# A decoder layer on one core: the first two block products of each gate and up pair are put ahead of the plain group before them, and the x loads get the priority of weight loads

## The chip, the cores and the metric

The kernel runs on one core of a Trainium2 chip. The metric is device time in microseconds; lower is better. A core has a matrix engine (TensorE, PE in the profile, with its weight loads as PEld), a vector engine (DVE), a scalar engine (ACT), GpSimd (POOL) and a sync engine (SP) that here issues most of the DMA transfers. Each engine works through its own instructions in the order in which the program has them; semaphores order them across engines.

## The reference

One layer on 256 tokens of width 2048, all in float32:

```
x = x + 0.5 * swiglu(rms_norm(x), ffn1 gate, up, down)     # 2048 -> 5632 -> 2048
x = x + hybrid_mixer(rms_norm(x), ...)                     # dilated attention || gated linear attention
x = x + cross_attention(rms_norm(x), rms_norm(mem), ...)
x = x + 0.5 * swiglu(rms_norm(x), ffn2 gate, up, down)

def swiglu(h, w_gate, w_up, w_down):
    return (jax.nn.silu(h @ w_gate) * (h @ w_up)) @ w_down
```

The change is in the two feed-forward blocks (FFN) and in one helper at the start. The mixer and the cross-attention between them stay as they are.

## The kernel before, in words

**Precision.** A float32 operand is held as a high part and a low part, both of type float32r. `split` (lines 137 to 139) makes them of a weight tile: ACT copies the tile to `wh`, DVE subtracts `wh` from it and writes `wl`. A product is then three matmuls: high by high, high by low, low by high. Activations are split the same way (`xTh` and `xTl`, `hTh` and `hTl`).

**Groups.** A weight matrix is read in tiles of 1 MB, 128 rows by 4 x 512 columns: four k blocks of one chunk of 512 output columns. One such tile used in the ordinary way is called a plain group here: `wgroup` loads and splits it, `mm3` (lines 160 to 168) does 4 k blocks x 2 token tiles x 3 = 24 matmuls. `proj` runs all the groups of a chunk one after the other.

**Pairs.** For chunk f = 0 of an FFN gate and up are two ordinary projections. For the other ten chunks `strassen` (line 201) computes gate and up of the chunk together. The k blocks of groups 0 and 1 of both matrices form a 2 x 2 block product (two token tiles by gate and up), done with seven block products (`product`, lines 191 to 199, 12 matmuls each) in place of eight. For that, weight tiles are added to each other: on DVE (`add`, line 215) and by DMA transfers that accumulate, which GpSimd issues (`accumulate`, line 219). `sums` (`sh`, `sl`) are the sums of activations, made once per FFN. Groups 2 and 3 of both matrices follow as four plain groups. PE's order in a pair is:

| step | matmuls | what |
|---|---|---|
| H1 (into `x`) | 12 | gate tile of group 0 |
| H2 (into `y`) | 12 | that tile plus the up tile of group 0 |
| turn of the chunk before | 8 transposes | its `h` becomes `hT` |
| P3 to P6 | 4 x 12 | further sums, up and gate tiles |
| G2 | 24 | gate, group 2 |
| P7 | 12 | last sum |
| U2, G3, U3 | 3 x 24 | up group 2, gate group 3, up group 3 |

Then ACT applies silu to gate (`sg`, line 375) and DVE multiplies with up (`h`, line 386).

**Parts.** The 11 chunks go in parts of 4, 4 and 3 (`PARTS`). After each part its `hT` tiles go through the down projection: four output chunks of 4, 4 or 3 plain groups. So two parts in each FFN begin with a pair behind a down projection.

**Buffers.** The split tiles `wh` and `wl` lie in rings of three buffers each. Loaded tiles (`raw`) have six buffers in two pools that take turns. In the accumulators' memory the tags `acc` and `ps` have four buffers each; H1 and H2 use `ps`, P4 and P6 accumulate into `acc`.

**What sets the order.** A planner orders each engine's instructions when the program is built, by the order of the code and by priorities: what stands in `tc.high_priority(200)` (`WPRI`: weight loads, splits, copies of the pairs) is moved forward as if it stood 200 instructions earlier. `later` and `tick` put off transposes by a number of products. Nothing is chosen at run time: an instruction that waits holds up all behind it on its engine.

**Start.** `load_x` (lines 444 to 450) reads the four 512 KB pieces of x, squares them on ACT and makes `r1`, the scale by which the norm is applied after the projection; silu of chunk 0 needs it. Its loads have priorities of 170, 136, 102 and 68.

## Time and profile before

| what | us |
|---|---|
| median of 3 runs | 1942.17 (1941.89 to 1942.6) |
| the profiled execution's own time | 1941.39 |
| its span, first to last instruction | 1939.6 |
| PE busy | 1920.4 (99%) |
| PE weight loads busy | 1584.2 (82%) |
| DVE busy | 1258.6 (65%) |
| ACT busy | 976.4 (50%) |
| GpSimd busy | 88.6 (5%) |

The 1.8 us between the profiled execution's time and its span lie around the instructions. Times in the profile count from the span's start. A recorded matmul of 512 columns lasts 0.39 us, and the next one can start while it still runs, so the distance from start to start shows more than the busy share. The first FFN lasts up to about 724 us, the second from about 1226 us to the end. The table of waits gives engine, tile and line, whom it waited for, and then total us, number of times and the longest; `xN` at a row's end merges N instructions of one kind.

### The profile page before, as it was taken

The page shows a single profiled execution, that of the slowest core. Times are in us where ns is not written, and L with a number is a line of the kernel's source. Part 1 is how long each engine was busy: PE and PEld are TensorE (multiplying, and loading weights), DVE is VectorE, ACT ScalarE, POOL GpSimd, SP SyncE. Part 2 cuts the span into 40 slices and gives each one's busy share as a digit, 9 for nine tenths or more (in the row PEclk, how much of TensorE's full clock was granted, in tenths as well). Part 3 has the DMA queues.
Part 4 walks back from the last instruction along what each step waited for, and adds up shares of the span by engine and source line. Part 5 has one row for each costly group of instructions (what it writes and reads, how often), then busy time and mean ns, then how long its engine had stood idle before and what let it go on. Part 6 is the DMA issues. An engine that isn't in the chain of part 4 may idle for free.

```text
span 1939.6 us, 21252 instructions
## 1 busy us (share of the span) xinstructions
PE 1920.4 (99%) x8760; PEld 1584.2 (82%) x8760; DVE 1258.6 (65%) x956; ACT 976.4 (50%) x881; POOL 88.6 (5%) x95
## 2 busy tenths in 40 slices
PE   9999999999999999999999999999999999999999
PEld 7888878888878888778888889888887888887887
DVE  7776477775578565446775555777646777557863
ACT  6555345553355446444566445555534555335642
POOL 0000000000000000012220000000000000000000
PEclk9999999999999999999999999999999999999999
DMA  9767557775477734445456553667755777556771
GB/s 380 247 220 282 188 177 264 270 250 195 152 236 249 274 127 156 158 162 190 174 217 217 176 193 132 253 224 239 260 195 154 264 269 268 194 174 217 238 290 57
DMA packets 63292, 416.13 MB, mean 215 GB/s; under 512 B 7099, under 2 KB 8251, under 8 KB 14428
## 3 DMA queue, kind: packets, MB, share of 16 engines
q1 hardware_dynamic: 55996, 370.22, 50.0%
q0 software_dynamic: 5760, 41.95, 10.5%
q10 hardware_dynamic: 1440, 2.62, 0.4%
q8 instruction: 68, 1.11, 0.2%
q14 instruction: 28, 0.23, 0.0%
HBM read 370.72 MB, written 2.10 MB: 192 GB/s over the span
## 4 chain that ended last, share of the span: by engine, by line
PE 73%; DVE 16%; ACT 6%; issue 4%; POOL 0%; DMA 0%; ACTq 0%; SPq 0%; DVEq 0%
PE acc L167 20%; PE acc L168 20%; PE acc L166 20%; DVE wl L139 11%; ACT wh L138 5%; PE x L197 4%; DVE raw L215 4%; PE x L167 1%; PE x L168 1%; PE x L166 1%; PE acc L197 1%; DVE acc L241 1%; DVE h L386 1%; PE y L197 1%; PE tp L313 0%
## 5 line engine op out<-in xcount | busy, mean ns | idle before, releaser
L139 DVE TENSOR_TENSOR wl<-raw,wh 128x2048 fp32r<-128x2048 f32 (+2 forms) x410 | 917.5, 2258 | 578.3 <-ACT wh L138 577.5
L138 ACT CAST wh<-raw 128x2048 fp32r<-128x2048 f32 (+2 forms) x410 | 762.9, 1886 | 646.2 <-PE acc L168 463.4
L166 PE MATMUL acc<-wh,xTh 128*128 128x512 f32 x1024 | 401.5, 394 | 7.2 <-ACT wh L138 7.2
L167 PE MATMUL acc<-wl,xTh 128*128 128x512 f32 x1024 | 401.1, 392 | 4.4 <-DVE wl L139 4.3
L168 PE MATMUL acc<-wh,xTl 128*128 128x512 f32 x1024 | 399.3, 390 | 0.0
L166 PE MATMUL acc<-wh,hTh 128*128 128x512 f32 x704 | 274.7, 390 | 0.0
L168 PE MATMUL acc<-wh,hTl 128*128 128x512 f32 x704 | 274.0, 389 | 0.0
L167 PE MATMUL acc<-wl,hTh 128*128 128x512 f32 x704 | 273.9, 389 | 0.0
L167 PEld LDWEIGHTS acc<-wl,xTh 128*128 128x128 f32 x1024 | 192.7, 188 | 50.8 <-DVE wl L139 11.9
L166 PEld LDWEIGHTS acc<-wh,xTh 128*128 128x128 f32 x1024 | 192.1, 188 | 49.5 <-ACT wh L138 9.4
L168 PEld LDWEIGHTS acc<-wh,xTl 128*128 128x128 f32 x1024 | 192.6, 188 | 39.8
L168 PEld LDWEIGHTS acc<-wh,hTl 128*128 128x128 f32 x704 | 132.1, 188 | 27.4
L166 PEld LDWEIGHTS acc<-wh,hTh 128*128 128x128 f32 x704 | 132.2, 188 | 27.2
L167 PEld LDWEIGHTS acc<-wl,hTh 128*128 128x128 f32 x704 | 132.2, 188 | 27.2
L215 DVE TENSOR_TENSOR raw<-raw 128x2048 f32<-128x2048 f32 x40 | 91.5, 2287 | 0.7
L219 POOL DMA_DIRECT2D raw<-raw x40 | 34.6, 865 | 1187.9 <-DVE raw L215 975.9
L167 PE MATMUL x<-wl,xTh 128*128 128x512 f32 x160 | 62.3, 389 | 0.0
L168 PE MATMUL x<-wh,xTl 128*128 128x512 f32 x160 | 62.3, 389 | 0.0
L166 PE MATMUL x<-wh,xTh 128*128 128x512 f32 x160 | 62.2, 389 | 0.0
L231 ACT COPY acc<-x 128x512 f32<-128x512 f32 x20 | 11.4, 571 | 95.6 <-PE x L197 95.6
L166 PE MATMUL acc<-wh,mTh 128*128 128x512 f32 x128 | 50.1, 392 | 0.0
L168 PE MATMUL acc<-wh,mTl 128*128 128x512 f32 x128 | 49.8, 389 | 0.0
(301 smaller groups left out, 1934.3 us busy)
## 6 DMA issues: line engine op xcount, KB each, us to landing
raw<-in_ffn_w_up_dram SPq DMA_DIRECT2D x88, 1024.0 KB, 7.7
raw<-in_ffn_w_down_dram SPq DMA_DIRECT2D x88, 1024.0 KB, 5.0
raw<-in_ffn_w_gate_dram SPq DMA_DIRECT2D x85, 1024.0 KB, 7.1
raw<-in_w_in_dram SPq DMA_DIRECT2D x48, 1024.0 KB, 4.8
raw<-raw POOLq DMA_DIRECT2D x40, 1024.0 KB, 6.9
raw<-in_w_out_dram SPq DMA_DIRECT2D x16, 1024.0 KB, 4.7
raw<-in_xattn_w_k_dram SPq DMA_DIRECT2D x4, 1024.0 KB, 5.2
raw<-in_xattn_w_q_dram SPq DMA_DIRECT2D x4, 1024.0 KB, 4.7
```

The costliest lines, as they stand in the source:

```text
L138: SC.copy(wh, src)
L139: last_split[:] = [V.tensor_sub(wl, src, wh.bitcast(F32)).ins]
L166: PE.matmul(acc[t], lh, wh, start=first and i == 0, stop=False, skip_group_check=seeded)
L167: PE.matmul(acc[t], lh, wl, start=False, stop=False, skip_group_check=seeded)
L168: PE.matmul(acc[t], ll, wh, start=False, stop=last and i == len(half) - 1, skip_group_check=seeded)
L197: PE.matmul(acc, lhs(k)[i], w[:, k], start=first, stop=j == 1 and k == 3, skip_group_check=not start)
L215: V.tensor_add(dst, x, y)
L219: G.dma_start(dst, x, accum_op=ALU.add)
L231: SC.copy(c0l, x)
L241: V.tensor_sub(c0r, ys, x)
L386: V.scalar_tensor_tensor(h, upv[t], r[:, t:t + 1], sg[t], op0=ALU.mult, op1=ALU.mult)
```

## The change

`strassen` is cut in two. `head` does the four loads, H1, H2 and the copies of their results, and returns a function `rest` that does P3 to U3. A caller can hand `ahead` to `proj` or `rest`: it is called just before the last plain group is written, and starts the head of the next pair there. That last group is U3 of the pair before, the last up group of chunk 0, or the last down group of a part. The last pair of a part has no such call; the down projection behind it makes it. The x loads go from their four priorities to `WPRI`.

```diff
-XPRI = 170
...
     def strassen(Wl, cl, Wr, cr, lhs, ab, sums, groups):
 
+        state = head(Wl, cl, Wr, cr, lhs, ab, sums)
+        return state(groups)
+
+    def head(Wl, cl, Wr, cr, lhs, ab, sums):
+
         a, b = ab
         ral, rar = load(Wl, cl, a), load(Wr, cr, a)
         rbr, rbl = load(Wr, cr, b), load(Wl, cl, b)
...
         x, y = PM([P, 512], "x"), PM([P, 512], "y")
-        c0l, c0r, c1r = (pa.tile([P, 512], F32, tag="acc", name="acc") for _ in range(3))
+        c0l = pa.tile([P, 512], F32, tag="acc", name="acc")
         product(x, of(a, 0), parts(ral), True)
...
-        add(ral, ral, rbr)
-        product(x, s_(1), parts(ral), False)
...
+        def rest(groups, ahead=None):
+            c0r, c1r = (pa.tile([P, 512], F32, tag="acc", name="acc") for _ in range(2))
+            add(ral, ral, rbr)
+            product(x, s_(1), parts(ral), False)
...
+            accs = ((c0l, x), (c0r, c1r))
+            for i, g in enumerate(groups):
+                for acc, W, c in zip(accs, (Wl, Wr), (cl, cr)):
+                    if ahead and acc is accs[1] and i == len(groups) - 1:
+                        ahead()
+                    for h, half in enumerate(wgroup(W, c, g)):
+                        mm3(acc, lhs, half, False, i == len(groups) - 1 and h == 1, seeded=True)
+                        tick()
+                    if i == 0 and W is Wl and c == cl:
+                        product(x, of(b, 1), parts(ral), False)
+            return accs
+
+        return rest
...
-    def proj(W, c, lhs, groups, fine=None, last=False):
+    def proj(W, c, lhs, groups, fine=None, last=False, ahead=None):
...
         for i, g in enumerate(groups):
+            if ahead and i == len(groups) - 1:
+                ahead()
...
+        def begin(f):
+            heads[f] = head(wg, f, wu, f, lhs_x, (0, 1), sums)
+
         for part in PARTS:
             for f in part:
+                ahead = (lambda f=f: begin(f + 1)) if f + 1 in part else None
...
-                    gate, upv = strassen(wg, f, wu, f, lhs_x, (0, 1), sums, (2, 3))
+                    gate, upv = heads.pop(f)((2, 3), ahead)
...
-                    upv = proj(wu, f, lhs_x, range(4))
+                    upv = proj(wu, f, lhs_x, range(4), ahead=ahead)
...
             for c in range(NC):
-                acc = proj(wd, c, lhs_h, part, last=last and end and c == NC - 1)
+                ahead = (lambda: begin(part[-1] + 1)) if c == NC - 1 and not end else None
+                acc = proj(wd, c, lhs_h, part, last=last and end and c == NC - 1, ahead=ahead)
...
-            with tc.high_priority(XPRI - 34 * c):
+            with tc.high_priority(WPRI):
                 SY.dma_start(xs[c], A["x"][0, :, c * 512:(c + 1) * 512].rearrange("(t p) d -> p t d", p=P))
```

Three places show what the planner makes of it. First DVE from chunk 2 to chunk 3 of the first FFN, before. `wl_962` is the split of G3, `wl_992` of U3, `wl_1041` and `wl_1060` of H1 and H2, `wl_1095` of P3, `wl_1112` of P4; the L215 rows are the two adds, the `h` rows the multiplication with up:

```order
L139 TENSOR_TENSOR wl_962<-raw_959,wh_961 128x2048
L139 TENSOR_TENSOR wl_992<-raw_989,wh_991 128x2048
L139 TENSOR_TENSOR wl_1041<-raw_1027,wh_1040 128x2048
L215 TENSOR_TENSOR raw_1027<-raw_1027,raw_1029 128x2048
L139 TENSOR_TENSOR wl_1060<-raw_1027,wh_1059 128x2048
L386 SCALAR_TENSOR_TENSOR h_1023<-acc_760,r1_323,sg_1019 128x512
L386 SCALAR_TENSOR_TENSOR h_1025<-acc_761,r1_323,sg_1021 128x512
L215 TENSOR_TENSOR raw_1027<-raw_1027,raw_1031 128x2048
L139 TENSOR_TENSOR wl_1095<-raw_1027,wh_1094 128x2048
L139 TENSOR_TENSOR wl_1112<-raw_1033,wh_1111 128x2048
```

And now; `wl_962` is G3 again, `wl_1001` and `wl_1020` are H1 and H2, `wl_1040` is U3, `wl_1079` P3, `wl_1096` P4:

```order
L138 TENSOR_TENSOR wl_962<-raw_959,wh_961 128x2048
L138 TENSOR_TENSOR wl_1001<-raw_989,wh_1000 128x2048
L219 TENSOR_TENSOR raw_989<-raw_989,raw_991 128x2048
L138 TENSOR_TENSOR wl_1020<-raw_989,wh_1019 128x2048
L219 TENSOR_TENSOR raw_989<-raw_989,raw_993 128x2048
L138 TENSOR_TENSOR wl_1040<-raw_1037,wh_1039 128x2048
L138 TENSOR_TENSOR wl_1079<-raw_989,wh_1078 128x2048
L138 TENSOR_TENSOR wl_1096<-raw_995,wh_1095 128x2048
L405 SCALAR_TENSOR_TENSOR h_1071<-acc_797,r1_323,sg_1067 128x512
L405 SCALAR_TENSOR_TENSOR h_1073<-acc_798,r1_323,sg_1069 128x512
```

U3's split has moved from ahead of H1's to behind the second add, and the `h` rows from ahead of the second add to behind P4's split.

Second SP in the first microseconds, before. `raw_254` is the last gate tile of chunk 0, `raw_347`, `raw_377`, `raw_407` and `raw_437` its up tiles, `raw_471` the first tile of chunk 1:

```order
L132 DMA raw_254<-in_ffn1_w_gate_dram 128x2048
L132 DMA raw_347<-in_ffn1_w_up_dram 128x2048
L448 DMA x0_103<-in_x_dram 128x2x512
L132 DMA raw_377<-in_ffn1_w_up_dram 128x2048
L448 DMA x1_104<-in_x_dram 128x2x512
L132 DMA raw_407<-in_ffn1_w_up_dram 128x2048
L132 DMA raw_437<-in_ffn1_w_up_dram 128x2048
L448 DMA x2_105<-in_x_dram 128x2x512
L132 DMA raw_471<-in_ffn1_w_gate_dram 128x2048
```

And now; `raw_437` to `raw_443` are the four tiles of the head of chunk 1:

```order
L131 DMA raw_254<-in_ffn1_w_gate_dram 128x2048
L468 DMA x0_103<-in_x_dram 128x2x512
L468 DMA x1_104<-in_x_dram 128x2x512
L468 DMA x2_105<-in_x_dram 128x2x512
L468 DMA x3_106<-in_x_dram 128x2x512
L131 DMA raw_347<-in_ffn1_w_up_dram 128x2048
L131 DMA raw_377<-in_ffn1_w_up_dram 128x2048
L131 DMA raw_407<-in_ffn1_w_up_dram 128x2048
L131 DMA raw_437<-in_ffn1_w_gate_dram 128x2048
L131 DMA raw_439<-in_ffn1_w_up_dram 128x2048
L131 DMA raw_441<-in_ffn1_w_up_dram 128x2048
L131 DMA raw_443<-in_ffn1_w_gate_dram 128x2048
```

All four x loads now stand ahead of the first up tile, and the head's four tiles ahead of the last up tile of chunk 0 (the row behind these).

Third ACT at the same time, before, from the last gate cast on. `junk` rows are the squares of x, `sh` rows the casts of the activation sums, `wh_349` and `wh_379` the casts of the first and second up tile:

```order
L138 CAST wh_256<-raw_254 128x1024 x2
L138 CAST wh_349<-raw_347 128x2048
L302 ACTIVATE junk_300,ss1_298<-x0_103 128x512
L302 ACTIVATE junk_302,ss1_298<-x0_103 128x512
L138 CAST wh_379<-raw_377 128x2048
L302 ACTIVATE junk_305,ss1_298<-x1_104 128x512
L302 ACTIVATE junk_307,ss1_298<-x1_104 128x512
L138 CAST sh_329<-sa_335 128x1024
L138 CAST sh_329<-sb_336 128x1024
L138 CAST wh_409<-raw_407 128x2048
```

And now, behind the last gate cast and the squares of x0 and x1:

```order
L315 ACTIVATE junk_310,ss1_298<-x2_105 128x512
L315 ACTIVATE junk_312,ss1_298<-x2_105 128x512
L315 ACTIVATE junk_315,ss1_298<-x3_106 128x512
L315 ACTIVATE junk_317,ss1_298<-x3_106 128x512
L137 CAST sh_329<-sa_335 128x1024
L137 CAST sh_329<-sb_336 128x1024
L394 ACTIVATE sg_325<-acc_128,r1_323 128x512
L394 ACTIVATE sg_327<-acc_129,r1_323 128x512
L137 CAST wh_349<-raw_347 128x2048
L137 CAST wh_379<-raw_377 128x2048
```

The first up cast stood right behind the last gate cast; now eight squares, two casts of sums and the two silus of chunk 0's gate stand between them.

## The prediction

> **Names.** A pair is the gate and up product of one chunk f of 512 hidden columns. In the order of the text before it has seven block products of 12 matmuls (H1 and H2, the ones that move; then P3 to P6; P7 after the first plain group) and four plain groups of 24 (G2, U2, G3, U3). Every weight tile is split first: ACT writes `wh`, DVE writes `wl`, into rings of three buffers.

> **What bounds the kernel now.** The page's first section:

> ```profile
> PE 1920.4 (99%) x8760; PEld 1584.2 (82%) x8760; DVE 1258.6 (65%) x956; ACT 976.4 (50%) x881; POOL 88.6 (5%) x95
> ```

> PE bounds it nearly everywhere, so the change can only win what PE loses between matmuls. The chain of waits shows the undisturbed pace, and the length of a pair:

> ```profile
> 118.31 2.72 PE x L197 x12
> 160.58 2.72 PE x L197 x12
> ```

> Twelve matmuls in 2.72 us is 0.227 us each. The same place comes back after 160.58 - 118.31 = 42.27 us. A pair has 7 x 12 + 4 x 24 = 180 matmuls, 40.8 us, and eight transposes, so somewhat over half a microsecond is lost in it. PE's timeline in chunk 7 shows where:

> ```profile
> 412.05 0.39 PE L166 MATMUL acc<-wh,xTh 128*128 128x512 f32 x1
> 412.28 0.39 PE L166 MATMUL x<-wh,xTh 128*128 128x512 f32 x1
> 412.86 0.50 PE L167 MATMUL acc<-wl,xTh 128*128 128x512 f32 x1 [0.19 <-DVE wl L139]
> 413.19 0.39 PE L168 MATMUL acc<-wh,xTl 128*128 128x512 f32 x1
> ```

> This is the start of G2. The start at 412.86 comes 0.58 us after the one before it, 0.35 too late; the next loses 0.11. Together 0.46 us (the profile calls only 0.19 idle, since a recorded matmul lasts 0.39 while the next may start after 0.227). The first pair of a part, which follows a down projection, loses more, here in chunk 4, and the first pair of all loses its share a little earlier, between H2 and P3:

> ```profile
> 284.17 0.39 PE L166 MATMUL x<-wh,xTh 128*128 128x512 f32 x1
> 286.02 0.73 PE L166 MATMUL acc<-wh,xTh 128*128 128x512 f32 x2 [1.47 <-ACT wh L138]
> 286.59 0.40 PE L167 MATMUL acc<-wl,xTh 128*128 128x512 f32 x1
> ...
> 56.67 1.07 PE L197 MATMUL y<-wl,sh 128*128 128x512 f32 x4
> 58.41 0.96 PE L197 MATMUL x<-wh,sh 128*128 128x512 f32 x3 [0.67 <-ACT acc L231]
> ```

> Chunk 4: 286.02 - 284.17 - 0.23 = 1.62, and 0.11 behind it, 1.73 us. Chunk 1: 58.41 - 56.67 - 4 x 0.227 = 0.83, with 0.11 behind it 0.94 us. The table of waits gives the counts:

> ```profile
> PEld acc L167 <- DVE wl L139: 11.9, 19, 2.0
> PEld acc L166 <- ACT wh L138: 9.4, 6, 2.0
> PE acc L166 <- ACT wh L138: 7.2, 5, 1.6
> ```

> Five waits of PE for `wh`: one is the kernel's first matmul, four are the first pairs of a part (two parts in each FFN). The waits for `wl` hold the 15 ordinary pairs (20 pairs less those four and chunk 1). What the pair waits for is the row of splits, seen on DVE and ACT:

> ```profile
> 384.07 1.91 ACT L138 CAST wh<-raw 128x2048 fp32r<-128x2048 f32 x1 [4.43 <-PE acc L168]
> 390.72 1.91 ACT L138 CAST wh<-raw 128x2048 fp32r<-128x2048 f32 x1 [0.52 <-DVE raw L215]
> ...
> 386.01 2.29 DVE L139 TENSOR_TENSOR wl<-raw,wh 128x2048 fp32r<-128x2048 f32 x1 [3.67 <-ACT wh L138]
> 388.34 2.29 DVE L215 TENSOR_TENSOR raw<-raw 128x2048 f32<-128x2048 f32 x1
> 392.67 2.29 DVE L139 TENSOR_TENSOR wl<-raw,wh 128x2048 fp32r<-128x2048 f32 x1 [2.03 <-ACT wh L138]
> 396.20 2.28 DVE L215 TENSOR_TENSOR raw<-raw 128x2048 f32<-128x2048 f32 x1
> 400.51 4.49 DVE L139 TENSOR_TENSOR wl<-raw,wh 128x2048 fp32r<-128x2048 f32 x2 [2.03 <-ACT wh L138]
> 410.52 6.69 DVE L139 TENSOR_TENSOR wl<-raw,wh 128x2048 fp32r<-128x2048 f32 x3
> ```

> Split, add, split, add, split follow one another (cast to `wl` 1.94, `wl` to add 2.33, add to cast 2.38, cast to `wl` 1.95), and a block product is over in 2.72 us. So the head eats the lead that the plain groups (5.44 us for one 2.29 us split) had built up, and the last `wl` of the row, at 410.52 + 2.3 = 412.8, is late.

> **The change part by part.** No instruction is added or removed on any engine; they change places.

> *H1 and H2 ahead of the last plain group.* Between H2 and P3 there now lie 24 matmuls, 5.44 us. I test whether the row of splits then keeps up. The three-buffer ring lets H1's cast begin when P7 ends. From there on DVE's order (shown above with the change): 1.94 + 2.33 + 2.38 + 1.95 to H2's `wl`, then 2.29 for it, 2.29 for the second add and 2.29 for the `wl` of U3: 15.5 us. PE has U2, G3, H1 and H2 in that time and then one matmul of U3: 3 x 5.44 + 0.23 = 16.6 us. So 1.1 us is to spare at the tightest place. The next ones have more: P3's cast can start at H1's end, and its `wl` ends 4.2 us later, with 8.2 us of PE work between; at G2, where today's stall is, the cast starts at P4's end and `wl` 4.2 us later, with the transposes, P5 and P6 (over 6.2 us) between. The silu results and `h` operations stand after these on ACT and DVE, and the transposes stay behind P4. In a part's first pair the same ring holds, as the last down group takes U3's place. So I count all the stalls as gone: 15 x 0.46 + 4 x 1.73 + 0.94 = 6.9 + 6.9 + 0.9 = 14.8 us. Ends of this term: half of it, 7.4, if the 1.1 us is used up in part; 16.5 if the 0.1 us goes as well by which an ordinary pair is longer than its matmuls, transposes and stall account for (15 x 0.1).

> *Loads.* H's four loads now stand ahead of U3's in SP's queue. A load lands within

> ```profile
> raw<-in_ffn_w_up_dram SPq DMA_DIRECT2D x88, 1024.0 KB, 7.7
> ```

> and U3's takes the buffer of U2, free when U2 is split, before U2's matmuls start; from there to U3's cast PE has U2 and G3, 10.9 us. Cost 0, hidden by these groups; without that cover up to 7.7 us per pair.

> *The x loads.* All four (2 MB in all) now go before the first up group's load, and on ACT their eight squares, the two casts of the sums and the two silus of the first gate stand ahead of the first up group's cast. That cast feeds PE directly:

> ```profile
> 21.65 2.00 ACT L138 CAST wh<-raw 128x1024 fp32r<-128x1024 f32 x2 [0.81 <-DMA raw<-in_ffn_w_gate_dram]
> 24.15 1.91 ACT L138 CAST wh<-raw 128x2048 fp32r<-128x2048 f32 x1 [0.50 <-DMA raw<-in_ffn_w_up_dram]
> 25.96 0.63 ACT L302 ACTIVATE junk<-x 128x512 f32<-128x512 f32 x1
> 31.40 1.06 ACT L138 CAST sh<-sa 128x1024 fp32r<-128x1024 f32 x1
> 56.62 1.25 ACT L375 ACTIVATE sg<-acc,r 128x512 f32<-128x512 f32 x2
> ...
> 25.01 1.22 DVE L180 TENSOR_TENSOR fa<-xTh,xTl 128x1024 f32<-128x1024 f32 x1
> 27.28 2.28 DVE L139 TENSOR_TENSOR wl<-raw,wh 128x2048 fp32r<-128x2048 f32 x1
> 31.40 0.69 DVE L187 TENSOR_TENSOR sb<-fb,sa 128x512 f32<-128x512 f32 x1
> 54.61 0.15 DVE L333 TENSOR_REDUCE r1t<-ss 128x2 f32<-128x8 f32 x1
> ...
> 55.12 0.71 POOL L329 TENSOR_TENSOR r<-r1m,mhalf 128x2 f32<-128x2 f32 x1 [5.51 <-DVE r1m L335]
> ...
> 30.38 0.62 PE L166 MATMUL acc<-wh,xTh 128*128 128x512 f32 x2
> 30.83 0.39 PE L167 MATMUL acc<-wl,xTh 128*128 128x512 f32 x1
> ```

> 1 MB lands in 24.15 - 21.65 = 2.5 us there, so the last x lands near 26.7 and the up group near 29.2. ACT: squares from 23.65 on, 8 x 0.63 = 5.0, to 28.7. DVE: the sums end at 32.1 less the 2.2 us of the up group's `wl`, which now comes later: 29.9; then the reduction up to the end of POOL's power, 55.83 - 54.61 = 1.2: 31.1. ACT meanwhile casts the sums (2 x 1.0, from 29.2 to 31.2), then the silus, 1.15 to the next start: 32.3. The up group's cast ends at 34.2, its `wl` 2.3 us later, 36.6. PE's third matmul of that group starts at 36.6 instead of 30.83: **5.8 us lost**, paid once. It is hidden by nothing, since all later work is behind it. Lower end: the second silu cannot start before the gate's last matmul ends near 30.5; 0.6 + 1.91 + 2.3 later is 35.3, 4.5 us lost. Upper end: x landing 2 us later, 8 us.

> *Sum.* Against the profiled execution (span 1939.6, its own time 1941.39): 1941.4 - 14.8 + 5.8 = 1932.4. The median of the runs shown is 0.8 above the profiled execution, so 1933.2; I say **1933.2**.

> **The rivals.**

> *A, the clock.* In the wait at the start PE stands still from 30.5 to 34.3, 3.8 us. At the kernel's start matmuls ran at half pace:

> ```profile
> 8.24 0.63 PE L168 MATMUL acc<-wh,xTl 128*128 128x512 f32 x1
> 8.66 0.63 PE L166 MATMUL acc<-wh,xTh 128*128 128x512 f32 x1
> ```

> 0.43 instead of 0.227. If the wait brings that back for eight matmuls, 8 x 0.2 = 1.6 us more: 1934.8. For it: no wait in this trace is near 3.8 us; against: behind 284.17, 1.6 us, the pace is full at once. [...] Chance 0.15.

> *B, the stalls move.* The 1.1 us at U3 is partly used up, by hand-over delays that I read from one pair, and half the gain stays: 1942.2 - 7.4 + 5.8 = 1940.6. For it: the margin is 7% of the row. Against: every other link has over 1 us. Chance 0.12.

> *C, slower.* The row of splits between P7 and U3 takes longer than PE's 16.6 us, say because H's loads, now kept over a plain group, come late to the adds. Each microsecond over costs 20 us in 20 pairs; past 0.65 us over (17.2 instead of 15.5) the kernel is slower than 1946. At 1 us over: 1933.2 + 20 = 1953. Against: the buffers they take are free after P6, G2 and P7 at the latest, and from P7's split, ahead of P7's matmuls, to the second add lie over 13 us against 7.7. Chance 0.07.

> **How the numbers follow.** Forecast 0.60, A 0.15, B 0.12, C 0.07, and 0.06 for a cheaper start with a full gain (1942.2 - 16.5 + 4.5 = 1930.2). 0.2% is 3.9 us, about what these runs can tell from no change. Forecast, A and the cheap start are faster by more: 0.81. B lies within 0.2%: 0.12. C: 0.07. The range reaches from just under the cheap start, 1929.5, over the dear one (1942.2 - 14.8 + 8 = 1935.4) with a few stalls left, to 1938.5; about 0.8 lies in it.

> **What would show it.** Right: the pair's 42.27 us becomes about 41.8; no wait of PE for `wh` or `wl` at G2 and none over 0.3 us in a pair; one wait of some 4 us near 30.5 and a shorter one near 35, with the up group's third matmul near 36.6. Wrong: waits for `wl` at U3 about 5 us into the group after H2 (B, C); matmuls 0.43 us apart after 34 (A); PE running through 30 to 36, which would mean that ACT's order does not bind.

## The result, and the profile after

The change takes 1933.19 us (median of 5 runs, 1932.96 to 1933.82) against 1942.17 us before (5 runs, 1941.85 to 1942.6): a ratio of 0.9954, 95% interval 0.994 to 0.9969. The prediction was 1933.2. The profiled execution of the change takes 1933.82 us with a span of 1932.0. That the total agrees does not say that its terms do, so they are taken apart here. In one experiment (e8) two of ten runs took 2879.82 and 9818.56 us; its time below is that of the other eight.

The first section of the changed kernel's page, to be held against the one of before:

```profile
PE 1916.0 (99%) x8760; PEld 1589.1 (82%) x8760; DVE 1265.0 (65%) x956; ACT 981.6 (51%) x881; POOL 90.3 (5%) x95
```

The numbers of instructions are the same. DVE and ACT are busy a few us more with the same work; PE has 4 us less. The chain of waits of the changed kernel (start, length, what):

```profile
67.39 2.72 PE x L196 x12
70.11 2.72 PE acc L196 x12
73.71 2.74 PE x L196 x12
...
109.08 2.72 PE x L196 x12
111.80 2.73 PE acc L196 x12
115.40 2.75 PE x L196 x12
```

The same place comes back after 115.40 - 73.71 = 41.69 us; before it was 42.27. In a pair the chain now runs over PE nearly without a break. The table of waits of the changed kernel (total us, times, longest):

```profile
PE acc L165 <- ACT wh L137: 5.0, 3, 3.1
PE acc L166 <- DVE wl L138: 3.6, 3, 1.6
PE tp L675 <- DVE o L690: 1.1, 1, 1.1
```

The waits of the 15 ordinary pairs for `wl`, of the four part-opening pairs for `wh` and the one in chunk 1 are gone. The waits left for split weights lie in the first 40 us and, one of 1.6 us, at 1230 us at the start of the second FFN; that one is there before the change too. PE's timeline at the start of the changed kernel:

```profile
32.22 0.39 PE L167 MATMUL acc<-wh,xTl 128*128 128x512 f32 x1
35.70 0.88 PE L165 MATMUL acc<-wh,xTh 128*128 128x512 f32 x2 [3.09 <-ACT wh L137]
38.02 0.79 PE L166 MATMUL acc<-wl,xTh 128*128 128x512 f32 x1 [1.44 <-DVE wl L138]
38.62 0.63 PE L167 MATMUL acc<-wh,xTl 128*128 128x512 f32 x1
39.04 0.63 PE L165 MATMUL acc<-wh,xTh 128*128 128x512 f32 x1
39.47 0.63 PE L166 MATMUL acc<-wl,xTh 128*128 128x512 f32 x1
```

Here are the two waits that were foretold, somewhat later than foretold, and behind them matmuls 0.43 us apart, which was rival A.

For one account of all this I added up, from the starts of PE's matmuls, by how much each matmul of a projection or block product is more than 0.227 us ahead of the next start (0.113, half of it, for half-size ones). The table has the sums in us for the profile of each kernel; "later" is everything behind chunk 1, and 11 us of it are the same in every kernel. The lower rows are the experiments below.

| kernel | first gate (chunk 0) | first up (chunk 0) | chunk 1 | later |
|---|---|---|---|---|
| before | 1.8 | 0.0 | 1.3 | 27.7 |
| the change | 4.2 | 7.6 | 0.1 | 11.1 |
| the change, second profile (e10) | 2.2 | 8.0 | 0.1 | 11.1 |
| heads alone (e1) | 1.9 | 0.0 | 5.3 | 11.1 |
| x loads alone (e2) | 1.8 | 7.8 | 0.7 | 27.8 |
| squares behind the first up split (e3) | 2.1 | 2.2 | 1.6 | 11.1 |
| no head ahead of a down projection's end (e4) | 2.4 | 8.4 | 0.1 | 19.2 |
| heads, but none for chunk 1 (e5) | 2.2 | 0.0 | 1.3 | 11.1 |
| short operation behind the second add (e7) | 2.4 | 9.7 | 0.5 | 13.3 |
| long operation there (e8) | 1.9 | 8.0 | 1.6 | 23.4 |

Heads and x loads together gained 27.7 + 1.3 - 11.1 - 0.1 = 17.8 us in the pairs, not 14.8. The start lost 8.4 (second profile) to 10.0 us (first), not 5.8. The two misses cancel in the total; that they do is luck.

### The profile page after: what moved, and what is told of

Same layout as the page of the kernel before. It is cut to its first block, busy times and chain, and to the rows that moved or that the text cites. A ratio compares the mean times of both kernels' runs of the same rounds, so it can differ in the third digit from the quotient of the medians.

```text
span 1932.0 us, 21279 instructions
## 1 busy us (share of the span) xinstructions
PE 1916.0 (99%) x8760; PEld 1589.1 (82%) x8760; DVE 1265.0 (65%) x956; ACT 981.6 (51%) x881; POOL 90.3 (5%) x95
## 4 chain that ended last, share of the span: by engine, by line
PE 96%; DMA 1%; DVE 1%; ACT 1%; POOL 0%; issue 0%; SPq 0%; ACTq 0%; POOLq 0%
PE acc L166 22%; PE acc L167 22%; PE acc L165 22%; PE x L196 11%; PE acc L196 6%; PE y L196 3%; PE x L167 2%; PE x L165 2%; PE x L166 2%; DMA raw<-in_ffn_w_gate_dram 1%; PE tp L366 1%; DVE wl L138 0%; PE tp L326 0%; ACT wh L137 0%; POOL gsr L686 0%
## 5 line engine op out<-in xcount | busy, mean ns | idle before, releaser
L138 DVE TENSOR_TENSOR wl<-raw,wh 128x2048 fp32r<-128x2048 f32 (+2 forms) x410 | 920.4, 2259 | 537.8 <-ACT wh L137 536.4
L166 PE MATMUL acc<-wl,xTh 128*128 128x512 f32 x1024 | 400.7, 391 | 3.6 <-DVE wl L138 3.6
L167 PE MATMUL acc<-wh,xTl 128*128 128x512 f32 x1024 | 400.4, 391 | 0.0
L167 PE MATMUL acc<-wh,hTl 128*128 128x512 f32 x704 | 274.0, 389 | 0.0
L166 PE MATMUL acc<-wl,hTh 128*128 128x512 f32 x704 | 273.9, 389 | 0.0
L166 PEld LDWEIGHTS acc<-wl,xTh 128*128 128x128 f32 x1024 | 193.4, 189 | 45.1 <-DVE wl L138 5.4
L167 PEld LDWEIGHTS acc<-wh,xTl 128*128 128x128 f32 x1024 | 193.2, 189 | 40.6
L167 PEld LDWEIGHTS acc<-wh,hTl 128*128 128x128 f32 x704 | 132.1, 188 | 27.4
L166 PEld LDWEIGHTS acc<-wl,hTh 128*128 128x128 f32 x704 | 132.2, 188 | 27.2
L166 PE MATMUL x<-wl,xTh 128*128 128x512 f32 x160 | 62.2, 389 | 0.0
L167 PE MATMUL x<-wh,xTl 128*128 128x512 f32 x160 | 62.2, 389 | 0.0
L413 DVE SCALAR_TENSOR_TENSOR x<-acc,x 128x512 f32<-128x512 f32 x48 | 33.0, 688 | 27.2 <-PE acc L167 27.2
L167 PE MATMUL acc<-wh,mTl 128*128 128x512 f32 x128 | 49.8, 389 | 0.0
## 6 DMA issues: line engine op xcount, KB each, us to landing
raw<-in_ffn_w_up_dram SPq DMA_DIRECT2D x88, 1024.0 KB, 6.7
raw<-in_ffn_w_down_dram SPq DMA_DIRECT2D x88, 1024.0 KB, 4.8
raw<-in_ffn_w_gate_dram SPq DMA_DIRECT2D x85, 1024.0 KB, 4.8
raw<-in_w_in_dram SPq DMA_DIRECT2D x48, 1024.0 KB, 4.8
raw<-raw POOLq DMA_DIRECT2D x40, 1024.0 KB, 7.1
raw<-in_w_out_dram SPq DMA_DIRECT2D x16, 1024.0 KB, 4.8
raw<-in_xattn_w_k_dram SPq DMA_DIRECT2D x4, 1024.0 KB, 4.8
raw<-in_xattn_w_q_dram SPq DMA_DIRECT2D x4, 1024.0 KB, 4.8
```

Of the source, the lines that this page charges most:

```text
L138: last_split[:] = [V.tensor_sub(wl, src, wh.bitcast(F32)).ins]
L166: PE.matmul(acc[t], lh, wl, start=False, stop=False, skip_group_check=seeded)
L167: PE.matmul(acc[t], ll, wh, start=False, stop=last and i == len(half) - 1, skip_group_check=seeded)
L413: V.scalar_tensor_tensor(xs[c][:, t], acc[t], 0.5, xs[c][:, t], op0=ALU.mult, op1=ALU.add)
```

## The experiments

**Theory.** The heads win all the stalls in the pairs; the x loads cost the start, because ACT does squares, sums and silus ahead of the first up cast; the two are independent. **Rivals.** The start's loss may come from the heads' own loads, the pairs' gain may depend on the x loads, or the time may come from the clock. e1 to e5 take the two apart, e7 and e8 are to measure the margin at U3, e6, e9 and e10 the clock.

### e1: the heads alone

The x loads get their four old priorities back:

```diff
-            with tc.high_priority(WPRI):
+            with tc.high_priority(XPRI - 34 * c):
                 SY.dma_start(xs[c], ...)
```

> The change without its last edit: heads ahead of the last plain group, x loads with their old priorities. Theory: the heads win about 17 us in the pairs (from the two profiles: 0.57 us in each of 15 ordinary pairs, about 2.0 in each of 4 first pairs of a part, 0.9 in chunk 1), and the early x loads cost about 9 us at the start. Without them the first up group's cast stands right behind the last gate cast again, so PE runs through 30 us: 1942.2 - 17 = 1925, plus about 1 us, because the silus of chunk 0 come late and H1's result is copied behind them, which P4 of chunk 1 waits for: 1926. Rival: the early x loads are needed for the heads (the silus free the accumulator that the head takes), and without them chunk 1 waits so long that nothing is won: 1932 or more.

Measured: 1929.14 us (1928.18 to 1930.96), ratio 0.9937 (0.9924 to 0.9949). The start is as before, the later pairs keep the whole gain, but 3 us are missing. The profile has one wait that neither kernel had. A row of its table of waits:

```profile
PE x L197 <- ACT acc L236: 3.6, 1, 3.6
```

ACT's timeline there in e1:

```profile
57.55 1.90 ACT L138 CAST wh<-raw 128x2048 fp32r<-128x2048 f32 x1 [2.84 <-PE acc L168]
59.35 1.26 ACT L395 ACTIVATE sg<-acc,r 128x512 f32<-128x512 f32 x2
60.50 0.60 ACT L236 COPY acc<-x 128x512 f32<-128x512 f32 x1
```

PE's P3 in chunk 1 needs H1's result copied out of `x`. The copy goes into an `acc` buffer that chunk 0's gate still holds, so it needs the silu of that gate; the silu needs the norm's scale, which with late x loads is there at 57.3 us (POOL's power runs from 56.58, 0.72 us). And ACT has a weight cast ahead of the silu. In the kernel before that is P3's cast, and it runs at once; here it is P5's, and it waits until PE has left chunk 0's last up group. Silu and copy follow it one by one, and PE starts P3 at 61.15, 3.8 us late where the kernel before lost 0.8. Half pace follows (the granted clock is 0.83 from 60 to 70 us; 1.3 us more). So heads and x loads are not independent at this one place.

### e2: the x loads alone

The kernel before, with the one line of the x loads changed to `WPRI`.

> The kernel before with only the priority of the x loads changed. Theory: ACT's order puts squares, sums and silus ahead of the first up cast here too, so PE waits about 5.5 us behind the gate of chunk 0 and then runs some 9 matmuls at half pace (1.8 us): 1942.2 + 7.3 = 1949.5, up to 1951.5 if the 2 us that the changed kernel lost inside the gate phase belong to the change and not to chance. Rival (the prediction's own term): 5.8 us, 1948.0. Rival that the x loads are free: 1942.2.

Measured: 1949.67 us (1948.78 to 1950.96), ratio 1.0043 (1.0029 to 1.0056): 7.9 us slower than before. The start's loss belongs to the x loads; no head is needed for it. In the table the start loses 7.8 us, and chunk 1 gets 0.6 back, since the scale is there early.

### e3: the change, with squares and silus behind the first up tile's split

```diff
+                def late():
+                    nonlocal r
+                    with tc.issue_after(last_split[0]):
+                        make_sums()
+                        r = finish()
+                    silus()
...
+                    upv = proj(wu, f, lhs_x, range(4), ahead=ahead, mid=late if wait else None)
```

`finish` makes the squares and the scale, `mid` is called between the first and the second up tile.

> The change, but squares of x, sums and silus of chunk 0 may only be issued behind the split of the first up tile; x loads still have the priority of weight loads, though the planner now puts two of the four ahead of the first up tile. Theory: ACT's order is what costs. The up tile lands near 24.2 + 2.6 = 26.8, cast to 28.7, wl to 31.0, when PE wants it at 30.8: no wait. About 2 us come back at U3 of chunk 0, whose cast now stands behind a copy that waits for H1: 1942.2 - 17 + 2 = 1927. Rival, that the transfers ahead of the up tile cost: the wait at 30 us stays at 3 us or more, 1930 or more.

Measured: 1928.62 us (1928.16 to 1929.62), ratio 0.9933 (0.992 to 0.9945), 4.6 us better than the change. The first up tile loses 0.5 us instead of 8. Two things are other there: ACT's order, and the planner now lets only two x loads ahead of the first up tile. ACT's timeline of e3:

```profile
27.14 1.91 ACT L138 CAST wh<-raw 128x2048 fp32r<-128x2048 f32 x1 [3.46 <-DMA raw<-in_ffn_w_up_dram]
```

and of the change, in its second profile (e10):

```profile
31.46 1.25 ACT L394 ACTIVATE sg<-acc,r 128x512 f32<-128x512 f32 x2
32.61 5.49 ACT L137 CAST wh<-raw 128x2048 fp32r<-128x2048 f32 x3
```

In the change the cast waits for no load; it follows the silus, so ACT's order is what ends last there. But the loads are not far behind. In e10 the first up tile is issued behind the four x loads, at 16.58 us, and takes 14.1 us to land: it is there at 30.7, 1.9 us before the cast starts (in the first profile it is issued at 16.90 us and takes 12.8). With ACT free at that moment the third matmul would come at 30.7 + 1.9 + 2.3 = 34.9, so by this estimate the loads alone would cost about 4 of the start's 6 us. No run has the two causes apart. What e3 still loses is 1.65 us at the second up tile, whose `wl` stands behind the sums on DVE, and 1.6 around the last one.

### e4: the change without a head ahead of a down projection's last group

```diff
-                ahead = (lambda: begin(part[-1] + 1)) if c == NC - 1 and not end else None
+                ahead = None
...
+                    if f not in heads:
+                        begin(f)
                     gate, upv = heads.pop(f)((2, 3), ahead)
```

The first pair of a part then starts behind the down projection, as before.

> The change without the heads ahead of the last down group: the first pairs of the four later parts begin with their head and go on at once, the other pairs as in the change. Theory: each of the four loses its 2.0 us again, at the start of G2: 1933.2 + 8 = 1941. The prediction's price was 1.73 each: 1940.1. Rival: what the down groups gain comes from elsewhere (earlier loads), and less than half comes back: below 1937.

Measured: 1941.27 us (1940.49 to 1942.91), ratio 0.9998 (0.999 to 1.0007). The four heads are worth 1941.27 - 1933.19 = 8.1 us; in the table 19.2 - 11.1 = 8.1, 2.0 us each. The prediction had read 1.73 at one place. What is left for the 15 ordinary pairs is 27.7 - 19.2 = 8.6 us, 0.57 each where it had read 0.46.

### e5: the heads alone, none for chunk 1

e1, and in chunk 0 of the first FFN no head:

```diff
                     if callable(r):
                         r = r()
+                        ahead = None
                 else:
+                    if f not in heads:
+                        begin(f)
                     gate, upv = heads.pop(f)((2, 3), ahead)
```

> The heads alone, with the x loads at their four old priorities, but chunk 1 of the first FFN without a head ahead of chunk 0's last up group (its pair starts as in the kernel before); all other heads stay. Theory: the 3.6 us wait in chunk 1 of the run with the heads alone comes from ACT's order there (a weight cast, then the silus, then the copy of H1's result), and from nothing else. Then start and chunk 1 lose what they lose in the kernel before (0.9 us for the silu and some tenths), and the other pairs keep their whole gain, 16.6 us by the sum of PE's start distances: 1941.4 - 16.6 = 1924.8 in the profiled execution, a median near 1925.2. Rival: the wait belongs to the late scale of the norm, whatever stands around it, and stays at 3 to 4 us: 1929.

Measured: 1925.66 us (1925.45 to 1927.8), ratio 0.992 (0.9906 to 0.9934). The table of waits has the wait of the kernel before in place of the 3.6 us:

```profile
PE x L197 <- ACT acc L236: 0.7, 1, 0.7
```

This is the best kernel of the study, 7.5 us under the change and 16.2 under the kernel before. It needs no x loads at weight priority: these serve one of the 20 heads, the one for chunk 1, and cost 8 us to save 1.2 there.

### e7 and e8: the margin at U3

In the trace of the change the margin that the prediction had worked out as 1.1 us can be read off. DVE's timeline between chunk 5 and chunk 6 in the change (the first of the three `wl` is U3's):

```profile
393.34 2.29 DVE L219 TENSOR_TENSOR raw<-raw 128x2048 f32<-128x2048 f32 x1
395.78 6.83 DVE L138 TENSOR_TENSOR wl<-raw,wh 128x2048 fp32r<-128x2048 f32 x3 [0.15 <-ACT wh L137]
```

and PE's there:

```profile
399.03 0.39 PE L165 MATMUL acc<-wh,xTh 128*128 128x512 f32 x1
399.25 0.39 PE L166 MATMUL acc<-wl,xTh 128*128 128x512 f32 x1
```

U3's `wl` is ready at 395.78 + 2.29 = 398.07 and used at 399.25: 1.18 us. To see whether that is all the slack there is, both kernels put one more operation behind the second add:

```diff
             add(ral, ral, rbr)
+            with tc.high_priority(WPRI):
+                V.tensor_tensor(ral[:, 0:1], ral[:, 0:1], ral[:, 0:1], op=ALU.max)
```

e8 takes the whole tile instead of `[:, 0:1]`.

> The change, with one more DVE operation in each pair behind the second add and ahead of U3's split, 128x512, about 0.7 us; it leaves its values as they are. Theory: the prediction's margin at U3 of 1.1 us covers it, and nothing changes: 1933.2, at most 1 us more. Rival B of the prediction (the margin is used up by hand-overs): 20 pairs x 0.7 = 14 us more, 1947.

> The change, with the same added operation four times as large, 128x2048, 2.29 us. Theory: 2.29 us is 1.1 to 1.2 over the margin at U3, with 0.1 us behind the wait 1.2 to 1.3 in each of 20 pairs: 24 to 26 us more, 1957 to 1959. Rival: the three buffers and the eight matmul groups of a pair hold more lead than the prediction counted, and the time stays under 1940.

Measured: 1934.90 us (1934.59 to 1936.33), ratio 0.9967 (0.9955 to 0.9979), with the short one, and 1946.07 us (1945.47 to 1947.67), ratio 1.0023 (1.0013 to 1.0034), with the long one. The short one takes 0.69 us and costs 0.1 us per pair on the mean, and the ordinary pairs pay nothing, though in ten of them DVE does it ahead of U3's split as meant (in 5 of the 20 places the planner put it behind the last group's split). What is paid lies at the last plain group of chunk 0 and of the part-opening pairs. PE's timeline of e7 in chunk 4, one of those:

```profile
316.44 0.39 PE L165 MATMUL acc<-wh,xTh 128*128 128x512 f32 x1
317.11 0.50 PE L166 MATMUL acc<-wl,xTh 128*128 128x512 f32 x1 [0.27 <-DVE wl L138]
```

In the change itself the margin at this place is 1.19 us too: `wl` is ready at 312.38 + 2.29 = 314.67 and used at 315.86. What makes it smaller in e7 is seen on ACT: the cast of the head's first tile, at 300.89, waits 1.37 us for that tile's load, and in the other three part-opening pairs 1.05 to 1.60 us (555.10, 1510.06, 1764.15); the change has no such wait. Why the load comes later there was not followed.

The long one loses 13.7 us in the pairs, 0.69 in each on the mean, about half of the 1.2 expected. But it did not test what it was meant to. The planner, which knows of the added operation when it builds the program, put it ahead of the last group's split in only five of the 20 places (chunk 0 of the first FFN, chunks 1 and 2 of both) and behind that split in the other fifteen. The five lose 4.3 us together, 0.65 to 0.85 in each of the four ordinary pairs. The four part-opening pairs lose 6.1 together, each at a late split a few us behind an ACT cast that has waited 1.5 to 2.05 us for an accumulating transfer (`raw<-raw`); that this wait is the cause was not tested. DVE's timeline of e8 at the end of chunk 1's pair, one of the five:

```profile
99.94 2.29 DVE L247 TENSOR_TENSOR raw<-raw 128x2048 f32<-128x2048 f32 x1
102.15 4.48 DVE L138 TENSOR_TENSOR wl<-raw,wh 128x2048 fp32r<-128x2048 f32 x2
```

and PE's there:

```profile
103.31 0.61 PE L165 MATMUL acc<-wh,xTh 128*128 128x512 f32 x2
104.28 0.73 PE L196 MATMUL x<-wh,sh 128*128 128x512 f32 x2 [0.36 <-ACT wh L137]
104.86 0.39 PE L166 MATMUL acc<-wl,xTh 128*128 128x512 f32 x1
```

U3's `wl` comes at 104.4, 0.9 us late where 1.1 to 1.2 was expected, and PE loses 0.65. The planner has changed PE's order as well: a second matmul of U3 and two of P3 stand ahead of the first one that needs `wl`, and PE works on those for part of the time. The expectation had taken both orders as fixed. Here a late split costs less than one for one; what a late split would cost in all 20 pairs was not measured.

### e6, e9, e10: the clock at the start

e10 is the change itself once more; e6 and e9 put idle work into the start wait, 14 and 26 matmuls (`FILL`):

```diff
+                        fill = PM([P, P], "fill")
+                        with tc.issue_after(last_mm[0]):
+                            for i in range(FILL):
+                                PE.matmul(fill, mhalf, mhalf, start=True, stop=True)
                     upv = proj(wu, f, lhs_x, range(4), ahead=ahead)
```

> The change, with 14 more matmuls of 128x128 (0.21 us each, 3.0 us together, their result is not used) on PE between the first gate's last matmul and the up group, so that PE works through most of its 3.2 us wait. Theory: the half pace behind 38 us (nine matmuls, 0.2 us each) follows from a wait of over 3 us, and it goes: 1933.2 - 1.8 = 1931.4, with matmuls 0.23 apart behind 38. Rival: the second wait, 1.8 us for the low parts, is enough for it, or the half pace comes with the place: 1933.2.

> The change, with 26 added matmuls of 128x128 in the start wait instead of 14 (0.235 us each by the run before, 6.1 us together; their result is not used). With 14, PE still stood still twice for 1.6 us between 33.8 and 37.7, and the half pace lasted 3.4 us instead of 6.8. Theory: the half pace follows from how much PE stands still there, in all, not from one long wait; with about 1 us left of both waits it does not come, and eight matmuls at 0.2 us are saved against the run with 14: 1932.6 - 1.6 = 1931.0, and matmuls 0.23 apart from the up group's third on. Rival: the added small matmuls do not count as work, and the half pace stays: 1932.6 or more.

> The change itself, unaltered, beside the run with the filled waits, so that both stand on one chip: 1933.2. In its profile the start should again show two waits near 30 to 38 and half pace behind them; whether a third stretch of half pace comes at 15 to 19 us, as in the first profile of the change, is open: by the mean clocks of the runs (0.997 or 0.998) it comes in some executions and not in others.

| run | us | half pace behind the wait |
|---|---|---|
| the change (e10) | 1933.60 (1932.30 to 1933.88) | 6.8 us |
| 14 matmuls (e6) | 1932.62 (1931.47 to 1933.03) | 3.4 us |
| 26 matmuls (e9) | 1931.14 (1931.04 to 1931.45) | none |

The last column is from the windows of 2 us of each kernel (busy time of PE, PEld, DVE, ACT and POOL, then the granted clock, DMA share, GB/s); the sum of 1 minus clock times 2 us is the loss, twice that the half pace. e10:

```profile
34.00:36.00 2.00, 1.22 (x2) 0.50 (x2) 1.47 (x1) 2.00 (x2) 0.00 (x0) 0.58 1.03 434
36.00:38.00 2.00, 1.13 (x3) 0.93 (x4) 2.00 (x2) 2.00 (x2) 0.00 (x0) 0.50 0.99 418
38.00:40.00 2.00, 2.00 (x6) 1.55 (x5) 2.00 (x2) 0.10 (x1) 0.00 (x0) 0.50 1.05 442
40.00:42.00 2.00, 2.00 (x8) 1.61 (x7) 1.22 (x1) 0.00 (x0) 0.00 (x0) 0.72 0.97 401
```

e6:

```profile
36.00:38.00 2.00, 0.41 (x2) 0.29 (x2) 2.00 (x2) 2.00 (x2) 0.00 (x0) 1.00 1.00 422
38.00:40.00 2.00, 2.00 (x6) 1.53 (x6) 2.00 (x2) 0.93 (x1) 0.00 (x0) 0.54 1.02 430
40.00:42.00 2.00, 2.00 (x7) 1.56 (x6) 2.00 (x1) 0.00 (x0) 0.00 (x0) 0.60 1.02 422
```

e9:

```profile
36.00:38.00 2.00, 1.28 (x9) 0.85 (x8) 2.00 (x2) 2.00 (x2) 0.00 (x0) 1.00 1.00 422
38.00:40.00 2.00, 2.00 (x10) 1.59 (x10) 2.00 (x2) 0.98 (x1) 0.00 (x0) 1.00 1.02 430
```

In e9 ACT and DVE deliver no sooner, the up group's third matmul starts at 37.76 (in e10 at 36.87, in the first profile at 38.02), and the kernel is 2.5 us faster than e10 beside it. Part of the 2.5 may be a stretch of half pace ahead of the wait, which comes in some executions (below). The two profiled executions have none there: 1932.30 - 1931.19 = 1.1 us, with the third matmul 0.9 us later in e9. So the added work saves 2.0 us behind the wait, the price of the half pace there. e6 did not bear out its theory: with the long wait cut to two of 1.6 us one of the two stretches of half pace came all the same. So here a single long wait was not needed; e9, by the same account, was foretold at 1931.0.

In the first profile of the change the granted clock is at one half from 15.64 to 19.05 us, which is 3.41, from 36.12 to 42.95, which is twice that, and from 1930.52 to the end of its record; in the kernel before, whose record begins at 10.11, only from 1938.64 on. Between the first two stretches it is full for 17.07 us, five times 3.41. By the windows of the other profiles up to 70 us (1 minus clock times the length, summed, twice) it is at one half for 3.4 us in e1, e3 and e6, 6.8 in e2, e4, e8 and e10, and 10.2 in e7. In the two traces the half clock follows stretches of 3.41 us in which PE is busy for 0.42 us (32.71 to 36.12) and 1.77 (12.23 to 15.64), and the ends, where it does next to nothing (0.11 and 0.02). It does not follow the stretch of the kernel before that holds the wait of 1.6 us at 1230 us and 1.83 us of PE work (1228.67 to 1232.09). In e1 it does not follow one with 1.73 either (1920.82 to 1924.24), so PE's busy time alone does not tell the two kinds apart, and what else does was not shown. In e6, where the clock falls near 38.2 us, PE is busy for 1.2 of the 3.4 us ahead.

e10's profile is also the cleaner one of the change. The start there, on PE:

```profile
30.29 0.39 PE L167 MATMUL acc<-wh,xTl 128*128 128x512 f32 x1
34.55 1.22 PE L165 MATMUL acc<-wh,xTh 128*128 128x512 f32 x2 [3.87 <-ACT wh L137]
36.87 0.80 PE L166 MATMUL acc<-wl,xTh 128*128 128x512 f32 x1 [1.10 <-DVE wl L138]
...
41.23 0.39 PE L165 MATMUL acc<-wh,xTh 128*128 128x512 f32 x1
```

The wait foretold at "some 4 us near 30.5" is 4.0, and the third matmul comes at 36.87 where 36.6 was foretold: 6.0 us behind the kernel before. From there to 41.23 PE does ten matmuls in 4.36 us, 2.1 more than at full pace. And the first gate loses 0.4 us, not the 2.4 of the first profile: there PE waited at 12 to 15 us for a gate tile's split (1.1 and 0.5 us), and ran at half clock for the 3.4 us behind it, in the windows of that first profile:

```profile
12.00:14.00 2.00, 0.89 (x4) 0.33 (x3) 0.46 (x1) 1.53 (x3) 0.00 (x0) 1.00 1.04 415
14.00:16.00 2.00, 1.48 (x6) 0.97 (x5) 2.00 (x4) 1.95 (x4) 0.00 (x0) 0.91 1.05 421
16.00:18.00 2.00, 2.00 (x6) 1.58 (x5) 2.00 (x4) 1.98 (x4) 0.00 (x0) 0.50 1.04 429
18.00:20.00 2.00, 2.00 (x8) 1.53 (x8) 2.00 (x4) 1.75 (x4) 0.00 (x0) 0.74 1.00 420
```

e10 has full clock in these windows, with the same program: there PE did 12 matmuls from 5 to 10 us (18 in the first profile), came later to that tile and hardly waited for it. So this third stretch, some 1.7 us, belongs to the execution and not to the change.

## Why the prediction was right, point by point

**PE bounds the kernel, and the change can win only what PE loses between matmuls.** Right: e5's profiled execution is 15.9 us shorter than the one of before, for 16.6 less between PE's starts in the pairs and 0.4 more in the first gate.

**H1 and H2 ahead of the last plain group: 14.8 us.** The mechanism was right in every detail that could be read: no wait at G2, none in a pair, the row of splits keeps up with 1.18 us to spare for 1.1 worked out, and by e7 that margin is real: 0.69 us more in the row cost nothing in ten ordinary pairs. The size was not right: 17.8 us, over the term's own upper end of 16.5 (14.8 + 15 x 0.1 is 16.3; 16.5 takes 0.11). The step that failed is "together 0.46 us" and "1.62, and 0.11 behind it, 1.73 us", as measures of what a pair loses. Both were read at one matmul, the one that waits. A pair lost 0.57 and a part-opening pair 2.0 (e4), because PE also lost in places that no row marks as a wait: 0.08 us behind the turn, and in P3 to P6 of a part-opening pair some ns at every matmul. Two rows of the chain of the kernel before, at such a pair, show it: the same twelve matmuls that take 2.72 us elsewhere.

```profile
1484.15 2.72 PE x L197 x12
1486.87 2.72 PE y L197 x12
1495.19 2.77 PE x L197 x12
1497.96 2.76 PE acc L197 x12
```

That is 15 x 0.11 + 4 x 0.28 + 0.2 (chunk 1) = 3.0 us. The pair's period would have given it: the prediction had 42.27 us and a count of 180 matmuls and eight transposes, called the rest "somewhat over half a microsecond", and then went on with the 0.46 of one place, with the difference kept only as an upper end.

**Loads: 0.** Right for the change: no wait for a weight load in any of its pairs. But the 7.7 us is the median from issue to landing and not an upper end, and in the part-opening pairs of e7 the head's load did come late.

**x loads: 5.8 us.** Right by 0.2 in the undisturbed start (e10: 6.0), and e2 shows that the x loads cause it. That ACT's order ends last, as argued, is read in e10's rows. But the first up tile landed at 30.7 and not near 29.2 (29.7 in the first profile), so the loads alone would have cost most of it. And this term was only the wait.

**Rival A, the clock, 0.15.** It came true: half pace behind the wait, 2.1 us by PE's starts in e10 and 2.0 by e9 against e10, for 1.6 estimated. It was set up as another outcome of the whole; it is a term that belongs in the sum. The chance of 0.15 was far too low: all seven profiles with a wait of 3.1 to 4.7 us have half clock behind it, for 3.4 us in e1, 10.2 in e7 and 6.8 in the other five. That it would be eight matmuls was the author's estimate; no run shows it at this wait, and e10 has ten in 4.36 us.

**The sum by what was measured:** 1941.4 - 17.8 + 6.0 + 2.1 + 0.4 (first gate) = 1932.1; e10's profiled execution took 1932.3. The forecast of 1933.2 is right to a tenth in the median by luck: a gain 3.0 too small stood against a loss of 2.6 to 4.2 too small.

**Rivals B and C** did not come: no wait for `wl` at U3. How much each us past the margin costs, for which C counted 20, stays open: e8 made the row longer in five places only, and the kernel was then just slower than before. Loads that come late to the row, C's example of a cause, are seen in e7 and e8 in the part-opening pairs. **The cheap start** (1930.2) did not come either.

**Missed altogether:** that one head hangs on the x loads. The prediction priced chunk 1 as one of the stalls that the heads win. e2 shows that the early scale wins half of that one without any head (1.3 becomes 0.7), e1 that the head without the early scale makes it worse (5.3), and the change that both together win it (0.1).

## What to carry to other kernels

What a repeating block loses is its period less the count of its instructions; one marked wait is a lower bound, so the sum should start from the period. Behind a wait of PE of some microseconds the granted clock is to be looked up, since half pace there is a second term (here 2.1 us behind the 4.0 in e10), and a few idle matmuls in the wait can be worth more than they seem (26 saved 2.0 us in e9). When a change couples a large move with a small one that "makes room" for it, the small one should be priced by the single place it serves: here 8 us were paid at the start for one head of 20, which could simply be left out. And what an added operation does is to be looked up in the order that was built, on every engine: e8's stood where it was meant to in five places of 20.
